# Strassen–Winograd on one core: S3 x T3 multiplied plainly in the first group of the table, T3's sums placed behind it, and a new order for every group

## The chip, the cores and the metric

One core of a Trainium2 chip runs the whole program. The metric is the device time of one execution in microseconds (us); three executions of the kernel before took 1464.37 to 1465.89 us, with a median of 1464.87.

## What is computed

```python
cs = np.cumsum(x, axis=1)
diff = cs - np.concatenate([np.zeros((B, 1, D)), cs[:, :-1, :]], axis=1)
return np.matmul(diff, w).astype(np.float32)   # x: 8 x 2048 x 2048, w: 2048 x 2048
```

A running sum followed by the differences of its neighbours gives x back, so what has to be computed is x times w: 16384 rows of x, cut into 128 tiles of 128 rows, each times a 2048 x 2048 matrix.

## The kernel before, in words

The first 4 tiles are multiplied plainly, the next 4 by one level of Strassen–Winograd, the next 4 by a mixture (`group_half`). From tile 12 on, 29 **groups** of four tiles each are worked through by a table. A group at tile g has the tiles g, h = g+2, k = g+1 and l = g+3. Tile g with tile k, and tile h with tile l, form the two row blocks of a 2 x 2 split: A11 and A12 are the two halves (of K) of g or h, A21 and A22 those of k or l. The matrix w, in 16-bit floats, is split into B11 to B22 and their sums T1 to T4, which stay in SBUF (named W). The seven outer products of a group are

- P1 = A11 x B11, P2 = A12 x B21, P3 = S4 x B22, P4 = A22 x T4, P5 = S1 x T1, P6 = S2 x T2, P7 = S3 x T3,
- where S1 = A21+A22, S2 = S1-A11, S4 = A12-S2, S3 = A22-S2, made in place by VectorE (DVE, L563, 128x1024).

P6 is multiplied plainly (L573): 32 matmuls in eight steps, P6g.0 to P6g.3 for tile g and P6h.0 to P6h.3 for h. The other six are split once more in the manner of Strassen–Winograd: seven quarter products `p1` to `p7` of 4 matmuls each (L592), 28 in place of 32, at the price of small sums of x (`s1` to `s4`, 128x512; six of them a group, listed in `ON_POOL`, run on POOL at L561, the others on DVE at L563), of copies on ScalarE (ACT, L1054, L1086), of merges in PSUM (`m1`, `a5g` and so on, L1061, DVE) and of sums of W. Those sums of W either lie ready (made once by `less`, L555, 128x2048) or are made anew in every group in a tile named flow by a *fill* (`fp4`, `fp5`..., L958, DVE). A group is 6 x 28 + 32 = 200 matmuls of 128x512.

T3's inner products need two sums that are made once, in place, on T3's own memory: T3 quarter 12 less quarter 11, then quarter 22 less that. In the kernel before both are made in the first group just ahead of P7's first fill.

The results of a product are read out of PSUM by `keep` (ACT, L600 with the row's scale, L1116 without) and later products are added by `add` (DVE, L603 with the scale, L1127 without). `last` (ACT, L600) then applies the scale where `add` did not, and `put` (L614) sends the 128x512 piece out. A tile of x comes in by `load` (L113, two transfers of 512 KB), its sizes are taken by `weigh0`, `weigh1` (ACT, L125), `scale` (POOL, L142), `recip` (DVE, L156), `unit` (POOL, L161), it is narrowed to 16 bits by `narrow0`, `narrow1` (ACT, L172) and transposed by two transfers, `turn0`, `turn1` (L185). All loads, turns and almost all puts are issued by SyncE (SP), in order.

What stands where on each engine is set by the string `ORDER`: 215 names, each with an offset of the group to which it belongs. For every group the loop goes through the string and issues each step to its engine; each engine then works in that order and waits by semaphores. Buffers (banks of PSUM, pieces c, the four scratch tiles of small sums) are handed out in that order as well. A load's two buffers are shared with the tile two places before it in the queue g, h, k, l, so load.k waits for turn1.g to land, load.l for turn1.h.

Of the kernel before, what the change touches and what calls it, by code (L numbers as in the profile page):

```python
# [10 lines left out]
def kernel(  # L11
# [1255 lines left out]
    ORDER = """  # L1267
    S1.h+0 S2.h+0 last.C12h1-1 put.C21h1-1 put.C12h1-1 last.C11g1+0 S4.h+0 keep.C22g0+0
    P3.p2+0 P6h.3+0 P5.s1+0 keep.C12g0+0 weigh0.g+1 add.C12g0.z+0 P6h.0+0 P6h.2+0
    P6h.1+0 weigh1.g+1 add.C11h0.q+0 S3.g+0 P5.s3+0 keep.C12g1+0 P7.p1+0 P4.p1+0  # L1270
    put.C11g1+0 P7.fp5+0 P3.s1+0 put.C11h0+0 S3.h+0 scale.g+1 recip.g+1 P7.s1+0 P7.c1+0
    P3.s3+0 P7.s2+0 put.C11h1+0 P7.a1+0 narrow0.g+1 P7.s3+0 P7.p5+0 P7.s4+0 P7.p6+0
    P7.p2+0 P7.fp7+0 keep.C12h1+0 P5.s2+0 P7.c5+0 P5.p5+0 keep.C21g0+0 P7.c6+0
    add.C22g0.x+0 P7.a5g+0 narrow1.g+1 P4.s1+0 P7.a5h+0 P5.s4+0 P5.ct+0 P7.a6+0 load.h+1
    P7.p7+0 P4.p2+0 add.C21g0.x+0 P4.s2+0 P5.p6+0 turn0.g+1 put.C21g0+0 P7.c7+0 P7.p3+0
    P3.s2+0 weigh0.h+1 P3.p1+0 P5.m1+0 P5.p3+0 weigh1.h+1 P7.a7h+0 put.C22g0+0
    add.C12g0.q+0 P5.fp4+0 P5.p7+0 last.C12g0+0 P3.s4+0 turn1.g+1 P3.p6+0 P4.p6+0
    keep.C22g1+0 P5.m2+0 P5.p4+0 scale.h+1 unit.l+0 add.C22g1.x+0 recip.h+1
    add.C12g1.q+0 keep.C12h0+0 P3.p7+0 P3.p3+0 P7.a7k+0 narrow0.h+1 keep.C22h0+0
    put.C12g0+0 keep.C22h1+0 narrow1.h+1 P7.fp4+0 add.C12h1.q+0 add.C12h0.q+0  # L1280
    add.C12h1.z+0 add.C22h1.x+0 P4.s3+0 unit.g+1 P7.p4+0 keep.C21h1+0 P3.p4+0 P4.p5+0
    P4.s4+0 add.C12h0.z+0 P3.p5+0 put.C22g1+0 keep.C21g1+0 P4.fp4+0 add.C12g1.z+0
    add.C22h0.x+0 add.C12g1.e+0 load.k+1 P4.p3+0 last.C12h0+0 weigh0.k+1 turn0.h+1
    P2.p1+1 P1.p1+1 weigh1.k+1 last.C12g1+0 turn1.h+1 P1.cg+1 add.C21g1.x+0 P1.s1+1
    scale.k+1 recip.k+1 put.C22h0+0 narrow0.k+1 put.C22h1+0 P4.p4+0 P1.s2+1 P1.p5+1
    add.C21g1.q+0 P1.s4+1 P2.s1+1 add.C21h1.e+0 P1.ct+1 put.C12h0+0 P2.s2+1 narrow1.k+1
    P1.p6+1 put.C12g1+0 keep.C11g0+1 P1.m1+1 P4.p7+0 add.C21h1.q+0 P1.p2+1 P1.s3+1
    P1.p3+1 load.l+1 P1.p7+1 unit.h+1 unit.k+1 P1.fp4+1 last.C21g1+0 keep.C21h0+0
    P2.s4+1 turn0.k+1 add.C21h0.x+0 P1.m2+1 keep.C11g1+1 P2.p6+1 add.C11g1.q+1 P2.cv+1
    weigh0.l+1 keep.C11h1+1 P2.s3+1 P2.p2+1 P2.p5+1 weigh1.l+1 P1.p4+1 add.C11g0.v+1  # L1290
    add.C11h1.e+1 turn1.k+1 last.C21h1+0 P2.p7+1 scale.l+1 put.C21h0+0 recip.l+1
    add.C12h1.e+0 S1.g+1 P2.p3+1 P5.p1+1 narrow0.l+1 S2.g+1 P2.fp4+1 P6g.0+1 P6g.1+1
    add.C11h1.q+1 narrow1.l+1 P2.p4+1 add.C11g1.e+1 P5.cg+1 P5.p2+1 put.C21g1+0
    put.C11g0+1 S4.g+1 P3.fp2+1 turn0.l+1 keep.C11h0+1 turn1.l+1 load.g+2 last.C11h1+1
    P6g.3+1 P6g.2+1
    """
# [72 lines left out]
```

## Time and profile before

| | us |
|---|---|
| median of three runs | 1464.87 |
| the profiled execution, whole | 1463.69 |
| its span (first to last instruction) | 1461.9 |
| PE busy, 6563 matmuls | 1428.8 |
| DVE busy, 2367 instructions | 1408.8 |
| ACT busy | 1160.6 |
| POOL busy | 356.6 |
| granted clock of TensorE over the span | 0.996 |

The profiled execution is 1.2 us shorter than the median of the runs and 1.8 us longer than its span. In the timeline a row merges neighbours of one kind; the figure behind x is how many, and a bracket tells how long the engine was idle before the row and who ended the wait. Times of a row count from the span's start. The table's 29 groups fill it from about 170 us on.

### The profile page before, as it was taken

What the parts mean: (1) busy time and instruction counts of PE and PEld (TensorE: products, weight loads), DVE (VectorE), ACT (ScalarE), POOL (GpSimd) and SP (SyncE); (2) the same over time, 40 slices, a digit from 0 to 9 for tenths busy, and PEclk for the clock granted to TensorE, in tenths of its full rate; (3) what the DMA queues carried; (4) which work ended last, traced back from release to release, by engine and by line L of the source; (5) the groups of instructions that cost most, each with busy time, mean ns of one, the idle gap of its engine ahead of it and who ended that gap; (6) DMA issues with size and microseconds to landing.
All of it is one profiled execution on the core that took longest, in us unless ns stands there. A gap on an engine that the chain in (4) does not pass through costs nothing. (4 is left out here: it accounts for less than half of the span.)

```text
span 1461.9 us, 21138 instructions
## 1 busy us (share of the span) xinstructions
PE 1428.8 (98%) x6563; PEld 635.8 (43%) x6563; DVE 1408.8 (96%) x2367; ACT 1160.6 (79%) x1786; POOL 356.6 (24%) x422
## 2 busy tenths in 40 slices
PE   8999989999999999999999999999999999999997
PEld 3444434444444444444444444444444444444443
DVE  7998899999999999999999999999999999999998
ACT  5887558888788888887888888887888887788882
POOL 0111021223231223321223321222321223221221
PEclk9999999999999999999999999999999999999999
DMA  9999839999898989889998899998889999889992
GB/s 358 368 237 298 213 121 237 240 232 252 228 244 232 250 228 251 236 237 239 238 238 247 238 230 251 251 228 240 241 239 239 252 229 243 229 245 245 248 243 105
DMA packets 377761, 351.65 MB, mean 241 GB/s; under 512 B 274800, under 2 KB 274800, under 8 KB 377520
## 3 DMA queue, kind: packets, MB, share of 16 engines
q1 hardware_dynamic: 377088, 348.47, 88.0%
q0 software_dynamic: 560, 1.84, 0.3%
q8 instruction: 51, 0.84, 0.2%
q14 instruction: 62, 0.51, 0.1%
HBM read 150.99 MB, written 134.22 MB: 195 GB/s over the span
## 5 line engine op out<-in xcount | busy, mean ns | idle before, releaser
L592 PE MATMUL b<-W,x 128*128 128x512 f16 x2124 | 522.3, 380 | 8.2 <-DVE x L563 6.1
L592 PEld LDWEIGHTS <-x 128*128 128x128 f16 x2952 | 286.5, 98 | 372.3 <-DVE x L563 19.6
L1127 DVE TENSOR_TENSOR c<-b,c 128x512 f32<-128x512 f32 x504 | 332.6, 678 | 0.6 <-issue 0.3
L172 ACT ACTIVATE F<-F,of 128x1024 f16<-128x1024 f32 x246 | 283.0, 1150 | 32.6 <-DVE of L156 30.8
L125 ACT ACTIVATE waste<-F 128x1024 uint8<-128x1024 f32 x246 | 259.9, 1057 | 54.5 <-DMA F<-in_x_dram 51.8
L592 PEld LDWEIGHTS <-inner 128*128 128x128 f16 x1996 | 192.6, 98 | 250.3 <-DVE inner L563 27.2
L592 PE MATMUL b<-W,inner 128*128 128x512 f16 x1176 | 288.9, 380 | 1.1 <-DVE inner L563 0.5
L573 PE MATMUL b<-W,x 128*128 128x512 f16 x1216 | 278.0, 379 | 0.3 <-DVE x L563 0.2
L563 DVE TENSOR_TENSOR x<-x,x 128x1024 f16<-128x1024 f16 (+1 forms) x359 | 211.9, 597 | 9.6 <-DMA x<-F 6.3
L603 DVE SCALAR_TENSOR_TENSOR c<-b,of,c 128x512 f32<-128x512 f32 x286 | 209.6, 740 | 8.9 <-PE b L592 5.5
L592 PE MATMUL b<-flow,x 128*128 128x512 f16 x820 | 210.4, 379 | 5.3 <-DVE flow L958 4.3
L600 ACT ACTIVATE c<-b,of 128x512 f32<-128x512 f32 x268 | 178.1, 681 | 37.9 <-PE b L592 13.7
L142 POOL TENSOR_SCALAR of<-of 128x1 f32<-128x1 f32 x112 | 79.5, 710 | 470.1 <-ACT waste L125 412.5
L1061 DVE TENSOR_TENSOR b<-b,c 128x512 f32<-128x512 f32 x290 | 191.6, 687 | 0.2 <-PE b L592 0.2
L1116 ACT COPY c<-b 128x512 f32<-128x512 f32 x224 | 128.5, 579 | 71.4 <-DVE c L603 45.0
L958 DVE TENSOR_TENSOR flow<-W 128x2048 f16<-128x2048 f16 x145 | 184.2, 1270 | 0.0
L573 PEld LDWEIGHTS <-x 128*128 128x128 f16 x1216 | 118.6, 98 | 144.7 <-DVE x L563 7.1
L600 ACT ACTIVATE c<-c,of 128x512 f32<-128x512 f32 x224 | 154.8, 714 | 12.9 <-DVE c L1127 12.9
L592 PE MATMUL b<-inner 128*128 128x512 f16 x472 | 121.1, 379 | 0.0
L561 POOL TENSOR_TENSOR inner<-x 128x512 f16<-128x512 f16 x29 | 35.7, 1232 | 268.2 <-PE b L592 268.2
L561 POOL TENSOR_TENSOR x<-x,x 128x512 f16<-128x512 f16 x58 | 88.3, 1522 | 22.3 <-PE b L592 22.3
L1086 ACT COPY c<-b 128x512 f32<-128x512 f32 x116 | 68.2, 588 | 26.8 <-PE b L592 17.9
(78 smaller groups left out, 988.9 us busy)
## 6 DMA issues: line engine op xcount, KB each, us to landing
F<-in_x_dram SPq DMA_DIRECT2D x246, 512.0 KB, 5.8
out_dram<-c SPq DMA_DIRECT2D x492, 256.0 KB, 3.2
W<-in_w_dram SPq DMA_DIRECT2D x32, 512.0 KB, 9.7
W<-in_x_dram SPq DMA_DIRECT2D x16, 256.0 KB, 7.1
x<-F SPq DMA_TRANSPOSE x246, 3.5
...
```

The costliest lines, as they stand in the source:

```text
L125: lambda: nc.scalar.activation(waste, where[t][i], ABS, scale=1.0 / ROW, accum_out=sums_of[t][:, i : i + 1],),
L172: lambda: nc.scalar.activation(narrowed(t)[:, ds(i * NH, NH)], where[t][i], COPY, scale=s),
L561: after("pool", lambda: nc.gpsimd.tensor_tensor(dst.all, p.all, q.all, op))
L563: after("dve", lambda: nc.vector.tensor_tensor(dst.all, p.all, q.all, op))
L573: said = nc.tensor.matmul(to[n], a[k], b[k][:, n, :], start=(first and k == 0), stop=(k == KH - 1), skip_group_check=True,)
L592: said = nc.tensor.matmul(to, a[k], b[k], start=(first and k == 0), stop=(k == 3), skip_group_check=True)
L600: after("act", lambda: nc.scalar.activation(c, p, COPY, scale=u))
L603: after("dve", lambda: nc.vector.scalar_tensor_tensor(c, p, u, c, MUL, ADD))
L958: after("dve", lambda: nc.vector.tensor_tensor(in_twos(flow), x, y, op))
L1061: after("dve", lambda: nc.vector.tensor_tensor(t, p, s, ADD))
L1116: after("act", lambda: nc.scalar.copy(to, p))
L1127: after("dve", lambda: nc.vector.tensor_tensor(to, p, to, ADD))
```

## The change

The diff, cut to what decides; of the table two lines of 29 stand for the rest.

```diff
-    ON_POOL = "P3.s1 P3.s4 P4.s1 P4.s3 P4.s4 P5.s4".split()
+    ON_POOL = "P2.s4 P3.s2 P4.s2 P4.s3 P4.s4 P5.s4".split()
...
-            self.small_sums("P7", A("g", 0), A("h", 0), True)
-            self.onto("P7", *x)
+            if self.more:
+                self.small_sums("P7", A("g", 0), A("h", 0), True)
+                self.onto("P7", *x)
+            else:
+                self.whole("P7", T3, half["g"][0], half["h"][0], *x)
...
     ORDER = """
-    S1.h+0 S2.h+0 last.C12h1-1 put.C21h1-1 put.C12h1-1 last.C11g1+0 S4.h+0 keep.C22g0+0
+    weigh0.l+1 keep.C11h1+1 P2.s3+1 P2.p5+1 weigh1.l+1 add.C11g1.q+1 last.C21h1+0
...
-    groups = [Group(g) for g in range(PLAIN + 8, END, 4)]
+    groups = [Group(g, g > PLAIN + 8) for g in range(PLAIN + 8, END, 4)]
...
+    PLAINLY = {
+        "P7.p5": ["P7g.0"],
+        "P7.p6": ["P7g.1"],
+        "P7.p2": ["P7g.2"],
+        "P7.p7": ["P7g.3"],
+        "P7.a7k": ["P7h.0", "P7h.1"],
+        "P7.fp4": ["P7h.2"],
+        "P7.p4": ["P7h.3"],
+    }
...
-first("P7.fp5", "P7.fp7", "P7.p6", "P7.fp4"): sums_of_T3
+"add.C12h1.e": lambda: less(in_7.t12, in_7.t12, in_7.t11)
+"add.C21h1.e": lambda: less(in_7.Q2, in_7.t22, in_7.t12)
```

Group 12, the first of the table, makes P7 with `whole`: 32 plain matmuls in eight steps P7g.0 to P7h.3, which stand where `PLAINLY` says. Its 28 quarter matmuls, four small sums, three fills, six merges and four copies for P7 are gone. Every other group makes P7 as before. `ORDER` is a new arrangement of the same 215 names (it also begins at another point of the circle), and three of the six sums on POOL are others.

What that does to an engine's rows is shown at three places. First DVE in group 12, around the start of P7. Of the rows before, x11 is S4.h, F is a sum of T1 for P5, c5 and c0 are adds, x00 is S3.g; the row of two W (128x4x512 x2) is the pair of T3's sums, flow the fill P7.fp5, and x10, the last row, S3.h.

```order
L563 TENSOR_TENSOR x11_66<-x11_66,x10_65 128x1024
L555 TENSOR_TENSOR F_62<-W_58 128x2048
L563 TENSOR_TENSOR inner_779<-x30_69 128x512
L1127 TENSOR_TENSOR c5_767<-b5_789,c5_767 128x512
L603 SCALAR_TENSOR_TENSOR c0_747<-b6_790,of_1280,c0_747 128x512
L563 TENSOR_TENSOR x00_63<-x21_68,x00_63 128x1024
L555 TENSOR_TENSOR W_58<-W_58 128x4x512
L563 TENSOR_TENSOR x30_69<-x20_67,x30_69 128x512
L555 TENSOR_TENSOR W_58<-W_58 128x4x512 x2
L958 TENSOR_TENSOR flow_783<-W_58 128x2048
L563 TENSOR_TENSOR x10_65<-x31_70,x10_65 128x1024
```

The same place in the changed kernel, from the sum for P5 (F) to add.C22g0.x, the row that reads PSUM bank b0:

```order
L555 TENSOR_TENSOR F_62<-W_58 128x2048
L563 TENSOR_TENSOR inner_779<-x30_69 128x512
L563 TENSOR_TENSOR x11_66<-x11_66,x10_65 128x1024
L563 TENSOR_TENSOR x00_63<-x21_68,x00_63 128x1024
L555 TENSOR_TENSOR W_58<-W_58 128x4x512
L563 TENSOR_TENSOR x30_69<-x20_67,x30_69 128x512
L563 TENSOR_TENSOR inner_779<-inner_779,x20_67 128x512
L563 TENSOR_TENSOR x20_67<-x31_70 128x512
L1128 TENSOR_TENSOR c5_767<-b2_786,c5_767 128x512
L563 TENSOR_TENSOR x10_65<-x31_70,x10_65 128x1024
L156 RECIPROCAL of_1655<-of_1655 128x1
L603 SCALAR_TENSOR_TENSOR c1_751<-b0_784,of_1320,c1_751 128x512
```

T3's pair, the fill and P7's small sums and merges have left this place; T3's sums now stand 17 and 28 rows behind the last row shown, ahead of add.C12h1.e and add.C21h1.e.

Second, ACT in a later group, around the weighing of the next tile k. Before: the last row of C12h0, then weigh0.k and weigh1.k (one row, x2), last.C12g1 (c2), a copy, narrow0.k, a copy, narrow1.k.

```order
L600 ACTIVATE c1_751<-c1_751,of_5848 128x512
L125 ACTIVATE waste_61,of_6317<-F_62 128x1024 x2
L600 ACTIVATE c2_755<-c2_755,of_5750 128x512
L1054 COPY b6_790<-b3_787 128x512
L172 ACTIVATE F_62<-F_62,of_6317 128x1024
L1054 COPY c0_747<-b4_788 128x512
L172 ACTIVATE F_62<-F_62,of_6317 128x1024
```

And now, with last.C12h1 (c5) between the weighings and keep.C21g1, a copy, narrow0.k, a copy, keep.C11g0, last.C12h0 (c4) and narrow1.k behind them:

```order
L600 ACTIVATE c2_755<-c2_755,of_5743 128x512
L125 ACTIVATE waste_61,of_6288<-F_62 128x1024
L600 ACTIVATE c5_767<-c5_767,of_5839 128x512
L125 ACTIVATE waste_61,of_6288<-F_62 128x1024
L1117 COPY c6_771<-b1_785 128x512
L1055 COPY b2_786<-b6_790 128x512
L172 ACTIVATE F_62<-F_62,of_6288 128x1024
L1055 COPY c2_755<-b4_788 128x512
L600 ACTIVATE c3_759<-b0_784,of_6116 128x512
L600 ACTIVATE c4_763<-c4_763,of_5839 128x512
L172 ACTIVATE F_62<-F_62,of_6288 128x1024
```

last.C12g1 has moved from behind both weighings to ahead of them. On SP the order is in both kernels four puts (put.C12g1 the last of them before, the first now), load.l, turn0.k, turn1.k.

Third, DVE in the same group around P7's last fill. Before: the fill P5.fp4, m2, add.C22g1.x, recip.h, add.C12g1.q, a7k, the fill P7.fp4.

```order
L958 TENSOR_TENSOR flow_783<-W_58 128x2048
L1061 TENSOR_TENSOR b2_786<-b3_787,c0_747 128x512
L603 SCALAR_TENSOR_TENSOR c4_763<-b4_788,of_5944,c4_763 128x512
L156 RECIPROCAL of_6221<-of_6221 128x1
L1127 TENSOR_TENSOR c2_755<-b5_789,c2_755 128x512
L1061 TENSOR_TENSOR b1_785<-b1_785,c6_771 128x512
L958 TENSOR_TENSOR flow_783<-W_58 128x2048
```

Now:

```order
L958 TENSOR_TENSOR flow_783<-W_58 128x2048
L156 RECIPROCAL of_6212<-of_6212 128x1
L1062 TENSOR_TENSOR b6_790<-b4_788,c1_751 128x512
L603 SCALAR_TENSOR_TENSOR c6_771<-b3_787,of_5915,c6_771 128x512
L1128 TENSOR_TENSOR c2_755<-b2_786,c2_755 128x512
L1062 TENSOR_TENSOR b7_791<-b7_791,c3_759 128x512
L958 TENSOR_TENSOR flow_783<-W_58 128x2048
```

recip.h has moved to directly behind the first of the two fills; the other rows kept their order.

More of the change, by code (lines that the diff above doesn't have):

```diff
@@ L1274 @@
[L1274 to L1295, printed above, removed]
+    weigh0.l+1 keep.C11h1+1 P2.s3+1 P2.p5+1 weigh1.l+1 add.C11g1.q+1 last.C21h1+0
+    scale.l+1 P2.fp4+1 add.C11h1.e+1 P2.p7+1 recip.l+1 add.C11h1.q+1 add.C21g1.x+0
+    put.C12h0+0 P2.p2+1 S1.g+1 S2.g+1 put.C21h1+0 P2.p3+1 narrow0.l+1 add.C11g1.e+1
@@ new lines @@
+    put.C21g1+0 P7.s2+1 P7.s3+1 P4.p1+1 recip.g+2 keep.C12g1+1 put.C21h0+0 P7.p5+1
+    P7.a1+1 P7.s4+1 load.h+2 P7.fp7+1 P7.c5+1 P7.a5g+1 P7.p6+1 P7.c6+1 P7.p2+1 P5.p5+1
+    P7.p7+1 add.C22g0.x+1 narrow0.g+2 P7.a6+1 P5.s4+1 P7.a5h+1 P3.s1+1 P4.p2+1 P4.s2+1
+    P5.p6+1 put.C22g0+1 keep.C21g0+1 narrow1.g+2 P7.c7+1 P7.p3+1 turn0.g+2 add.C21g0.x+1
+    P3.s3+1 P5.ct+1 P3.p1+1 put.C21g0+1 weigh1.h+2 P5.m1+1 P5.p7+1 P5.p3+1 P3.s2+1
+    weigh0.h+2 P7.a7h+1 P3.s4+1 scale.h+2 add.C12g0.q+1 P5.fp4+1 keep.C22g1+1 recip.h+2
@@ new lines @@
+    P3.p6+1 last.C12g0+1 P4.p6+1 P5.m2+1 unit.g+2 unit.l+1 keep.C12h0+1 keep.C22h1+1
+    add.C22g1.x+1 narrow0.h+2 P5.p4+1 add.C12g1.q+1 P3.p3+1 unit.h+2 P7.a7k+1 P7.fp4+1
+    P3.p7+1 turn1.g+2 put.C12g0+1 P7.p4+1 put.C22g1+1 add.C12h1.z+1 add.C12g1.z+1
+    add.C22h1.x+1 load.k+2 P3.p5+1 P4.s4+1 narrow1.h+2 keep.C22h0+1 turn0.h+2
+    add.C12h1.q+1 add.C12g1.e+1 keep.C21h1+1 last.C12g1+1 weigh0.k+2 P3.p4+1
+    add.C12h1.e+1 turn1.h+2 last.C12h1+1 add.C12h0.q+1 P4.s3+1 add.C22h0.x+1 P4.fp4+1
@@ new lines @@
+    P4.p3+1 P2.p1+2 put.C12g1+1 add.C12h0.z+1 weigh1.k+2 scale.k+2 P1.s1+2 P4.p5+1
+    P1.s3+2 recip.k+2 P1.s2+2 P1.p1+2 put.C22h0+1 keep.C21g1+1 add.C21g1.q+1 P1.cg+2
+    put.C12h1+1 put.C22h1+1 load.l+2 narrow0.k+2 add.C21h1.e+1 P1.s4+2 P4.p4+1 P1.p5+2
+    P1.ct+2 keep.C11g0+2 P1.p6+2 last.C12h0+1 P2.s1+2 P4.p7+1 narrow1.k+2 turn0.k+2
+    P1.m1+2 P2.s2+2 add.C21h1.q+1 P1.p2+2 P1.p7+2 turn1.k+2 keep.C21h0+1 P2.cv+2
+    P1.fp4+2 P1.p3+2 P1.m2+2 unit.k+2 keep.C11g1+2 P2.s4+2 P2.p6+2 P1.p4+2 add.C21h0.x+1
```

36 lines of the change are left out of this document (19 added, 17 removed).

## The prediction

> **What bounds the kernel now.** The page's first part comes first: which engine is full.
>
> ```profile
> span 1461.9 us, 21138 instructions
> PE 1428.8 (98%) x6563; PEld 635.8 (43%) x6563; DVE 1408.8 (96%) x2367; ACT 1160.6 (79%) x1786; POOL 356.6 (24%) x422
> ```
>
> PE and DVE are both full, so the view by stretches comes next: the whole of the table's steady part (from the start of P5.p1 in group 20 to that in group 124, 26 groups), then single groups, then the first.
>
> ```profile
> 279.70:1419.88 1140.18, 1129.49 (x5202) 503.67 (x5201) 1119.54 (x1925) 946.88 (x1483) 308.41 (x364) 1.00 0.91 240
> 411.24:456.10 44.86, 43.34 (x201) 19.43 (x201) 42.88 (x75) 37.62 (x58) 12.22 (x14) 1.00 0.93 237
> 456.10:499.40 43.30, 43.30 (x200) 19.47 (x201) 42.93 (x75) 35.20 (x57) 12.67 (x14) 1.00 0.89 240
> 543.82:587.09 43.27, 43.27 (x201) 19.42 (x201) 42.80 (x75) 36.41 (x58) 12.23 (x14) 1.00 0.94 245
> 191.00:235.50 44.50, 38.41 (x162) 15.85 (x159) 41.61 (x69) 29.00 (x47) 9.57 (x13) 0.92 0.67 182
> ```
>
> Columns: length, then busy time with count of PE, PEld, DVE, ACT, POOL, then granted clock, DMA share and GB/s. An undisturbed group lasts 43.3 us for 200 matmuls, 0.216 us each, and PE never idles; DVE idles 0.4 to 0.5 us in it. So PE sets the pace and DVE has hardly any room. The steady part averages 1140.18 / 26 = 43.85 us a group: 0.55 us a group, 14 us in all, is disturbance. The first group is worse: 162 matmuls where 200 would fit, at a granted clock of 0.92. Who PE waits for is in the view of waits.
>
> ```profile
> PE b L592 <- DVE inner L563: 6.4, 7, 4.3
> PE b L592 <- DVE x L563: 6.1, 8, 1.5
> PE b L592 <- DVE flow L958: 4.3, 8, 0.6
> ```
>
> Columns: us in total, times, longest. Three kinds of wait, 16.8 us of PE's 33; most of the rest lies in the head and the tail, which the change hardly touches.
>
> **Term A, the first group.** The timeline of PE and DVE shows it.
>
> ```profile
> 193.53 1.90 PE L592 MATMUL b<-W,x 128*128 128x512 f16 x8 [0.76 <-DVE x L563]
> 199.72 1.89 PE L592 MATMUL b<-flow,inner 128*128 128x512 f16 x4 [4.29 <-DVE inner L563]
> 201.40 1.91 PE L592 MATMUL b<-W,inner 128*128 128x512 f16 x4
> 206.09 1.03 PE L592 MATMUL b<-flow,x 128*128 128x512 f16 x4
> 215.37 1.02 PE L592 MATMUL b<-W,x 128*128 128x512 f16 x4 [0.28 <-DVE c L1127]
> 217.47 1.02 PE L592 MATMUL b<-flow,x 128*128 128x512 f16 x4 [0.21 <-DVE flow L958]
> 194.86 2.47 DVE L555 TENSOR_TENSOR W<-W 128x2048 f16<-128x2048 f16 x2
> 197.37 1.22 DVE L958 TENSOR_TENSOR flow<-W 128x2048 f16<-128x2048 f16 x1
> 198.51 0.68 DVE L563 TENSOR_TENSOR x<-x,x 128x1024 f16<-128x1024 f16 x1
> 199.58 0.42 DVE L563 TENSOR_TENSOR x<-x,x 128x512 f16<-128x512 f16 x1
> 199.91 0.42 DVE L563 TENSOR_TENSOR inner<-inner,x 128x512 f16<-128x512 f16 x1
> 822.75 1.88 DVE L1061 TENSOR_TENSOR b<-b,c 128x512 f32<-128x512 f32 x3
> ```
>
> At 199.72 PE starts P7.p5 after 4.29 us of idling: DVE first made T3's two sums (2.47 us) and the fill (1.22). Then 16 matmuls take from 199.72 to 206.09, 6.37 us in place of 16 x 0.216 = 3.5: 2.9 us more, in the stretch with the low granted clock. Both go: the plain product needs no sum of T3, no fill and no small sum, only S3.g and two banks. S3.g stands, in the new rows of DVE, 1.2 + 0.4 + 0.7 + 0.7 = 3 us behind S2.h, while PE has P6h's four steps and P4.p1 there (5 x 0.86 = 4.3), so nothing else is late there. The 0.76 ahead of it, for S3.g, falls with it, and the 0.28 and 0.21 as well, since P7 leaves DVE in this group with three fills (197.37 to 198.51, 1.14 each), four small sums (199.58 to 199.91, 0.33) and six merges (three in 1.88, 0.60 apart) less, 8.3 us. Gains: 4.3 + 2.9 + 0.8 + 0.5 = 8.5.
>
> Costs: 32 matmuls for 28, 4 x 0.216 = 0.9. P4.p2 follows P7g.3 directly on PE and adds into bank b0, which add.C22g0.x must read in between: one DVE add and two hand-overs.
>
> ```profile
> L603 DVE SCALAR_TENSOR_TENSOR c<-b,of,c 128x512 f32<-128x512 f32 x286 | 209.6, 740 | 8.9 <-PE b L592 5.5
> L600 ACT ACTIVATE c<-b,of 128x512 f32<-128x512 f32 x268 | 178.1, 681 | 37.9 <-PE b L592 13.7
> ```
>
> 0.74 and, for the hand-overs, an estimate of some 0.07 each (in the rows of term B a 0.7 us sum starts at 455.35 and PE, released by it, at 456.10), so 0.9. T3's sums are still made, 2.47 us, at the seam to the next group, where DVE can't have saved up the 8.3 us, because it reads what PE has just made. Bounds: 0 (hidden) to 2.5 (nothing hidden); nearest is the row of 543.82, whose DVE idles 0.47 us, so I take 1.7. A = -8.5 + 0.9 + 0.9 + 1.7 = **-5.0** (-6.7 to -4.2).
>
> **Term B, waits for tile k.** The 6.1 us behind "x L563" are, but for the 0.76 above, P5.p1 waiting for S1.g.
>
> ```profile
> 456.10 1.04 PE L592 MATMUL b<-W,x 128*128 128x512 f16 x4 [1.52 <-DVE x L563]
> 455.35 1.42 DVE L563 TENSOR_TENSOR x<-x,x 128x1024 f16<-128x1024 f16 x2 [1.51 <-DMA x<-F]
> 444.43 1.01 SPq L113 DMA_DIRECT2D F<-in_x_dram  x2
> 445.60 5.29 SPq L185 DMA_TRANSPOSE x<-F  x2
> L125 ACT ACTIVATE waste<-F 128x1024 uint8<-128x1024 f32 x246 | 259.9, 1057 | 54.5 <-DMA F<-in_x_dram 51.8
> ```
>
> DVE waited 1.51 us for k's transposes, PE 1.52 for DVE. SP issues load.l (1 MB) at 444.43 and both of k's turns right behind it, which take it 5.29 us: the transposes queue behind the load. In the new rows of ACT last.C12g1 stands ahead of two weighings of 1.06 us, so put.C12g1, ahead of load.l on SP, is free some 2 us earlier, the load with it, and k's transposes land earlier by up to as much; the string also names turn1.k six PE steps (5.2 us) ahead of S1.g, before one. No wait was over 1.52. Value: all of it, -(6.1 - 0.8) = **-5.3**; bounds 0 to -5.3.
>
> **Term C, the fill that meets a sum on POOL.** 4.3 us behind "flow" and 6.4 - 4.3 - 0.5 = 1.6 behind "inner" (0.5 is of the first group's start) are left, less 0.2 counted in A: 5.7.
>
> ```profile
> 371.97 2.15 DVE L563 TENSOR_TENSOR x<-x,x 128x1024 f16<-128x1024 f16 x3 [0.73 <-DMA x<-F]
> 391.61 2.09 DVE L958 TENSOR_TENSOR flow<-W 128x2048 f16<-128x2048 f16 x1
> 391.46 1.15 POOL L561 TENSOR_TENSOR x<-x,x 128x512 f16<-128x512 f16 x1 [0.50 <-PE b L592]
> 393.75 1.02 PE L592 MATMUL b<-flow,x 128*128 128x512 f16 x4 [0.65 <-DVE flow L958]
> 831.31 1.21 DVE L958 TENSOR_TENSOR flow<-W 128x2048 f16<-128x2048 f16 x1
> 831.34 2.20 POOL L561 TENSOR_TENSOR x<-x,x 128x512 f16<-128x512 f16 x1 [0.66 <-PE b L592]
> ```
>
> P7.fp4 on DVE and P4.s4 on POOL are let go by one and the same product, P5.p4. Where DVE starts no later (831.31), its fill takes 1.21 and POOL's sum 2.20. Where POOL is 0.15 ahead (391.46), the sum takes 1.15, the fill 2.09, and PE waits 0.65. DVE was late there because it had waited 0.73 us for tile l's transposes. In the new string turn1.l stands three PE steps ahead of S1.h, before two: 0.9 us more. That covers the 0.73 of this group, but the pair still starts on one event. Value: half, **-2.8**; bounds -5.7 and, where the fill loses more often, the rival below.
>
> [...]
>
> **Term D, undisturbed groups.** 43.3 us against 200 x 0.216 = 43.2: 0.1 us a group, 2.6 in all, can be won. What could be lost are DVE's own waits.
>
> ```profile
> DVE of L156 <- POOL of L142: 8.5, 35, 1.0
> ```
>
> `recip` waits for `scale` 8.5 us in all. In the new rows recip.h stands directly behind a fill, and load.h behind four puts, so it may wait anew; recip.g and recip.k now have sums of x between them and their `scale`. Bounds -2.6 and +2.6 (0.1 us a group either way); I take **+1.0**. ACT (79%), POOL (24%) and the tail's own fixed order are left at nothing; ACT's cover is the 5 to 8 us that it idles in a group.
>
> **Sum.** -5.0 - 5.3 - 2.8 + 1.0 = -12.1 on the profiled execution's 1463.69, 1451.6; the median lies 1.2 above that execution, so **1452.8**.
>
> **Rivals.**
> - *All waits of the table go*: A, B, all of C, D's 2.6: -5.0 - 5.3 - 5.7 - 2.6 = -18.6, 1446.3. For it: every one of them begins with a late transpose. Against: the pair on one event.
> - *Only the first group counts*: the transposes land as late as before, because DMA is at a share of 0.91 anyway: -5.0 + 1.0, 1460.9.
> - *The fill loses in every group*, the one that ends slower. The new rows put the chain P5.p3, keep.C22g1 (ACT, 0.68), add.C22g1.x, add.C12g1.q, a7k ahead of P7.fp4: 0.68 + 0.66 + 0.60 + 0.60 + two hand-overs 0.1 = 2.64 us from the end of P5.p3, while PE ends P5.p4 3 x 0.86 = 2.59 us after it. DVE and POOL are within 0.1 us of each other; from about 0.1 behind POOL's start DVE loses. It decides from about 20 lost groups on: 4.3 / 0.65, six waits, are there already, and 22 more of the 28 groups that keep the fill are 14.3, with C at nothing: -5.0 - 5.3 + 1.0 + 14.3 = +5.0, 1469.9. Against it: both wait for the same product, and a DVE that is there in time starts first (831.31 against 831.34), as it did in all but six groups.
> - *Half of them lose*: near 1462 to 1466, no change that a measurement shows (within 0.2%, 2.9 us, is about what one can tell here).
>
> **How the numbers follow.** Forecast 0.48, its own range 1447 to 1459; all waits go 0.14; only the first group 0.14; half lose 0.09; all lose 0.15. Faster by over 0.2%: 0.48 + 0.14 + 0.14 = 0.76; within: 0.09; slower: 0.15. The range runs from 1443, below the second case by its bounds, to 1468, into the cases where most fills lose, short of all of them: some 0.14 lies above, 0.04 below.
>
> **What would show it.** A: no wait over 1 us in group 12, no stretch with a granted clock of 0.92, a wait of about 0.9 ahead of P4.p2, and one of 1 to 2 us in all behind T3's sums. B: no wait of "x L563" for DMA at S1.g. C: the number of fills of 2.1 us at P7.fp4, six before; the slow rival needs over 20. D: undisturbed groups of 43.2 to 43.4 us. Wrong would be, above all, a group that lasts over 43.8 us with no late transpose in it.

## The result, and the profile after

The changed kernel took **1496.98 us** (median of 4 executions, 1495.37 to 1499.84), the kernel before on the same chip 1465.09 (1464.37 to 1465.89): a ratio of 1.0222, 95% interval 1.0203 to 1.024, 31.9 us slower. 1452.8 was predicted, and the range ended at 1468. The profiled execution took 1495.37, its span is 31.4 us longer than that of before. The page's first part:

```profile
span 1493.3 us, 21071 instructions
PE 1439.1 (96%) x6567; PEld 632.1 (42%) x6567; DVE 1424.4 (95%) x2354; ACT 1147.4 (77%) x1782; POOL 406.8 (27%) x422
```

DVE has 13 instructions fewer than before and is busy 15.6 us longer; POOL has as many as before and is busy 50 us longer. Somebody's instructions have become slower. Where, the view by stretches tells: the steady part (P5.p1 of group 20 to that of group 124), group 72, group 80, and the first group, now from its own P5.p1 to the next group's. Columns as in the prediction.

```profile
276.20:1453.59 1177.39, 1142.47 (x5201) 500.72 (x5201) 1145.22 (x1925) 936.19 (x1483) 353.49 (x364) 1.00 0.89 233
867.55:912.76 45.21, 43.91 (x201) 19.27 (x201) 44.44 (x75) 36.09 (x58) 13.50 (x14) 1.00 0.88 233
957.14:1002.38 45.24, 43.78 (x201) 19.28 (x200) 43.64 (x75) 35.93 (x58) 13.65 (x14) 1.00 0.89 233
183.47:231.31 47.84, 44.99 (x205) 19.74 (x204) 38.97 (x65) 33.24 (x52) 11.60 (x13) 1.00 0.65 177
```

The first group in the same stretch of the kernel before:

```profile
182.25:235.50 53.25, 47.16 (x202) 19.86 (x200) 49.27 (x78) 34.78 (x56) 11.08 (x13) 0.94 0.57 157
```

The first group is 5.4 us shorter. The steady part is 1177.39 - 1140.18 = 37.2 us longer, 45.28 us a group for 43.85. (The rest: head +1.2, the second group +0.7, the tail -2.3; in all 31.4.) DVE's share of it, with the same 1925 instructions: busy 1145.22 for 1119.54, **25.7 us more**; idle 32.2 for 20.6, **11.5 us more**. Both halves have to be explained. The view of PE's waits, columns us in total, times, longest:

```profile
PE b L592 <- DVE flow L958: 19.2, 29, 1.0
PE b L592 <- ACT c L1087: 9.6, 20, 1.1
PE b L592 <- DVE b L1062: 7.5, 16, 0.7
PE b L592 <- DVE inner L563: 1.6, 3, 0.6
PE b L592 <- DVE x L563: 0.4, 2, 0.2
```

The three kinds of before are nearly gone but for the fill, 8 times before and now 29; two new ones stand beside it. (A step's last matmul is drawn 0.17 us longer than the 0.86 us at which steps follow each other, so each wait costs some 0.17 us more than this view says.) Counted in the two traces from the start of one step to the start of the next, PE's steps of the steady part come 54.2 us late in all, for 17.0 before: the 37.2 us. Of them P7.p4 has 16.2 (21.1 for 4.9), P7.p6 12.5 and P5.p7 7.5, which lost nothing before; P5.p1 gives 5.3 back (2.9 for 8.2); the other 6.3 are small waits, most of them too short for the view. One group shows all three in a row. Here is group 72, DVE first, from P3.s3 to P7's last fill; a row without a bracket follows its predecessor without idling.

```profile
885.51 1.37 DVE L563 TENSOR_TENSOR x<-x,x 128x512 f16<-128x512 f16 x1
886.80 1.28 DVE L1062 TENSOR_TENSOR b<-b,c 128x512 f32<-128x512 f32 x2
888.00 0.41 DVE L563 TENSOR_TENSOR inner<-x,inner 128x512 f16<-128x512 f16 x1
888.33 0.68 DVE L1128 TENSOR_TENSOR c<-b,c 128x512 f32<-128x512 f32 x1
888.93 1.21 DVE L958 TENSOR_TENSOR flow<-W 128x2048 f16<-128x2048 f16 x1
...
891.98 0.68 DVE L1062 TENSOR_TENSOR b<-b,c 128x512 f32<-128x512 f32 x1
892.58 1.76 DVE L958 TENSOR_TENSOR flow<-W 128x2048 f16<-128x2048 f16 x1
```

POOL, PE and ACT beside it:

```profile
885.44 1.16 POOL L561 TENSOR_TENSOR inner<-inner,x 128x512 f16<-128x512 f16 x1 [1.05 <-PE b L592]
892.10 3.25 POOL L561 TENSOR_TENSOR x<-x,x 128x512 f16<-128x512 f16 x2 [1.56 <-PE b L592]
887.54 1.02 PE L592 MATMUL b<-W,x 128*128 128x512 f16 x4 [0.46 <-DVE b L1062]
890.99 1.03 PE L592 MATMUL b<-flow,x 128*128 128x512 f16 x4
894.39 1.02 PE L592 MATMUL b<-flow,x 128*128 128x512 f16 x4 [0.65 <-DVE flow L958]
876.19 1.06 ACT L125 ACTIVATE waste<-F 128x1024 uint8<-128x1024 f32 x1 [1.97 <-DMA F<-in_x_dram]
879.37 0.58 ACT L1087 COPY c<-b 128x512 f32<-128x512 f32 x1
880.00 1.02 PE L592 MATMUL b<-W,inner 128*128 128x512 f16 x4 [0.18 <-ACT c L1087]
885.58 0.60 ACT L1055 COPY c<-b 128x512 f32<-128x512 f32 x1
```

- 885.44: POOL's P3.s2 starts 0.07 us ahead of DVE's P3.s3 (885.51), which then takes 1.37 us in place of 0.42. That makes P5.m1 (886.80) late, and PE waits 0.46 for it at P5.p7 (887.54). So in 13 of the 27 groups between the first and the last.
- 886.80 to 892.58: from P5.m1 on DVE works without a break for 5.78 us and reaches the fill P7.fp4 at 892.58. PE let it and POOL's P4.s4 go at 892.02 (the end of P5.p4, 890.99 + 1.03). POOL started at 892.10; the fill takes 1.76 for 1.21 and PE waits 0.65. So in all 27 groups.
- 876.19: ACT had waited 1.97 us for load.g; the copy c1 (879.37), behind two weighings and two other rows, is late for PE's P7.p6 (880.00), which waits for c1 in most groups.

Of DVE's 25.7 us the rows by shape account for most: the 128x512 sums of x, of which P3.s3 is one in three, and the fills that read sums of T, one in five of them P7.fp4.

```profile
L563 DVE TENSOR_TENSOR x<-x,x 128x512 f16<-128x512 f16 x89 | 49.3, 555 | 0.1
L958 DVE TENSOR_TENSOR flow<-W 128x2048 f16<-128x2048 f16 x142 | 187.7, 1322 | 0.0
```

Before these groups had a mean of 415 and 1270 ns: 89 x 0.14 = 12.5 us and 142 x 0.052 = 7.4 us more. Of the 11.5 us of idling, 7.4 are DVE's waits for copies of ACT such as c1 (20 times, none before) and 1.7 more waits of recip. Whether these stretched rows are the cause, or only what a late DVE looks like, the trace alone does not say.

### The profile page after: what moved, and what is told of

Same layout as the page of the kernel before. It is cut to its first block, busy times and chain, and to the rows that moved or that the text cites. A ratio compares the mean times of both kernels' runs of the same rounds, so it can differ in the third digit from the quotient of the medians.

```text
span 1493.3 us, 21071 instructions
## 1 busy us (share of the span) xinstructions
PE 1439.1 (96%) x6567; PEld 632.1 (42%) x6567; DVE 1424.4 (95%) x2354; ACT 1147.4 (77%) x1782; POOL 406.8 (27%) x422
## 4 chain that ended last, share of the span: by engine, by line
PE 39%; DVE 25%; DMA 14%; ACT 10%; issue 9%; POOL 2%; SPq 1%; DVEq 0%; ACTq 0%
PE b L592 27%; PE b L573 9%; DVE c L1128 7%; DVE flow L958 6%; DMA out_dram<-c 6%; DMA F<-in_x_dram 5%; DVE b L1062 4%; ACT waste L125 4%; DVE c L603 3%; ACT c L600 3%; DVE x L563 2%; PE b L289 2%; DVE inner L563 2%; POOL of L142 2%; DMA W<-in_w_dram 2%
## 5 line engine op out<-in xcount | busy, mean ns | idle before, releaser
L592 PEld LDWEIGHTS <-inner 128*128 128x128 f16 x1984 | 188.6, 98 | 262.4 <-DVE inner L563 27.5
L600 ACT ACTIVATE c<-b,of 128x512 f32<-128x512 f32 x268 | 181.8, 684 | 81.5 <-PE b L592 44.6
L142 POOL TENSOR_SCALAR of<-of 128x1 f32<-128x1 f32 x112 | 64.2, 573 | 659.7 <-ACT waste L125 548.0
L592 PE MATMUL b<-flow,x 128*128 128x512 f16 x812 | 208.2, 379 | 20.5 <-DVE flow L958 19.2
L563 DVE TENSOR_TENSOR x<-x,x 128x1024 f16<-128x1024 f16 (+1 forms) x329 | 209.4, 651 | 5.9 <-DMA x<-F 3.6
L1117 ACT COPY c<-b 128x512 f32<-128x512 f32 x224 | 129.8, 580 | 84.2 <-DVE c L603 47.1
L958 DVE TENSOR_TENSOR flow<-W 128x2048 f16<-128x2048 f16 x142 | 187.7, 1322 | 0.0
L600 ACT ACTIVATE c<-c,of 128x512 f32<-128x512 f32 x224 | 160.3, 716 | 17.1 <-DVE c L1128 17.1
L561 POOL TENSOR_TENSOR inner<-x,inner 128x512 f16<-128x512 f16 x58 | 108.3, 1867 | 174.7 <-PE b L592 164.8
L561 POOL TENSOR_TENSOR x<-x,x 128x512 f16<-128x512 f16 x87 | 127.3, 1477 | 52.6 <-PE b L592 46.4
L161 POOL TENSOR_SCALAR of<-of,uw 128x1 f32<-128x1 f32 x124 | 65.6, 545 | 91.6 <-DVE of L147 81.4
```

The lines of the kernel that those rows point to most:

```text
L561: after("pool", lambda: nc.gpsimd.tensor_tensor(dst.all, p.all, q.all, op))
L563: after("dve", lambda: nc.vector.tensor_tensor(dst.all, p.all, q.all, op))
L592: said = nc.tensor.matmul(to, a[k], b[k], start=(first and k == 0), stop=(k == 3), skip_group_check=True)
L600: after("act", lambda: nc.scalar.activation(c, p, COPY, scale=u))
L958: after("dve", lambda: nc.vector.tensor_tensor(in_twos(flow), x, y, op))
L1117: after("act", lambda: nc.scalar.copy(to, p))
```

## The experiments

The expectations name the theories by letters. M: rows of DVE and POOL meet and stretch each other. Q: ACT waits for load.g, and DVE is late from the copy c1 on. K: the unbroken chain of DVE rows from P5.m1 to P7.fp4 is too long, so the fill loses. T: the new string loses the fills whatever POOL does. D: DVE is full, and a wait that is taken away comes back elsewhere. A: ACT is late because of load.g. The runs are numbered in the order in which they ran. Moves in the string are shown as a difference of its names. All ratios are to the kernel before on the same chip, with the 95% interval.

**1. Only the first group.** The string and POOL's list of before, with the plain first group; its steps and T3's sums stand where the old string leaves room. The lines are a difference to the changed kernel, without the string and the list.

```diff
         "P7.p6": ["P7g.1"],
-        "P7.p2": ["P7g.2"],
-        "P7.p7": ["P7g.3"],
+        "P7.p2": ["P7g.2", "P7g.3"],
         "P7.a7k": ["P7h.0", "P7h.1"],
-        "P7.fp4": ["P7h.2"],
-        "P7.p4": ["P7h.3"],
+        "P7.fp4": ["P7h.2", "P7h.3"],
...
-"add.C12h1.e": lambda: less(in_7.t12, in_7.t12, in_7.t11)
+"add.C12g1.e": lambda: less(in_7.t12, in_7.t12, in_7.t11)
```

> The table and the POOL sums of before; only the first group multiplies S3 x T3 plainly, with T3's sums behind it. Both theories expect the 4.29 us wait and the half-rate stretch of the first group to go: group 12 (P5.p1 to P5.p1 of the next) 53.3 us before, about 48 here, and the run about 5 us (0.3%) faster than before. If the first group's gain is paid back at the seam, the run is within 0.1% of before.

1457.51 us, ratio 0.9955 [0.994, 0.9971]: 6.6 us faster than the kernel before. The first group, and the steady part:

```profile
182.39:229.43 47.04, 44.79 (x206) 19.64 (x204) 39.48 (x65) 32.63 (x52) 10.63 (x13) 1.00 0.67 179
273.00:1413.91 1140.91, 1129.95 (x5201) 503.79 (x5201) 1118.19 (x1925) 947.43 (x1483) 307.92 (x364) 1.00 0.90 240
```

53.25 has become 47.04, the granted clock 1.00, and the other groups are as they were (1140.91 for 1140.18). The plain first group is a gain; everything lost is lost by the new order and the new list.

**5 and 6. The string alone, the list alone.** Run 5 is the changed kernel with the old list:

```diff
-    ON_POOL = "P2.s4 P3.s2 P4.s2 P4.s3 P4.s4 P5.s4".split()
+    ON_POOL = "P3.s1 P3.s4 P4.s1 P4.s3 P4.s4 P5.s4".split()
```

> The changed kernel with the six POOL sums of the kernel before: the new string and the plain first group stay. Theory K (the chain on DVE): what loses the fills P7.fp4 is the chain from P5.m1 to P7.fp4, 5.48 us of DVE rows in the kernel before against 6.04 us in which PE comes from P5.p6 to the end of P5.p4; P3.s4, moved from POOL into it, makes it 5.81, and P3.s3, stretched by POOL's P3.s2, starts it late. With the old list P3.s4 is off the chain and P3.s2 off POOL: most fills are won, P7.p4 waits under 6 us in all, P5.p7 under 2, the time 1465 to 1476. Theory T (the string alone): copies on ACT come late whatever POOL does, the fills are lost as before, P7.p4 waits about 20 us, 1485 or more.

Run 6 is the kernel before with the new list:

```diff
-    ON_POOL = "P3.s1 P3.s4 P4.s1 P4.s3 P4.s4 P5.s4".split()
+    ON_POOL = "P2.s4 P3.s2 P4.s2 P4.s3 P4.s4 P5.s4".split()
```

> The kernel before with the six POOL sums of the changed kernel: the old string, no plain first group. Theory K: P3.s4 on DVE leaves 0.2 us of the 0.56 spare, so fills are lost in most groups: P7.p4 waits 12 to 20 us in all, 1475 to 1485. Theory T: the list alone does little, within 4 us of 1465.

1497.45 (1.0235 [1.0212, 1.0259]) and 1499.86 us (1.0254 [1.0236, 1.0273]): **either half alone costs as much as both**, and either alone loses every fill. Of run 6:

```profile
PE b L592 <- DVE flow L958: 19.1, 29, 0.7
PE b L592 <- DVE b L1061: 7.4, 30, 1.1
279.00:1456.64 1177.64, 1141.40 (x5200) 499.52 (x5201) 1147.23 (x1925) 940.81 (x1483) 303.39 (x364) 1.00 0.87 233
```

Run 6 bears K out in the lost fills (P3.s4 has joined the chain), but its time lies 15 us above K's range: P7.p3 waits for a merge in every group as well (the second line), which I had not foreseen. Run 5 went as T said, but not against K: I had overlooked that with the old list the new string puts P3.s2 on DVE right behind P5.m1, inside the chain, where the old string has it ahead of P5.m1. In all three kernels the chain is one 0.33 us sum longer than before. How thin the margin of the kernel before is, its own rows show: the chain starts with this row, and ends at the fill of 831.31, 0.03 us ahead of POOL's sum (831.34).

```profile
825.87 1.29 DVE L1061 TENSOR_TENSOR b<-b,c 128x512 f32<-128x512 f32 x2
```

5.44 us, against 5.78 in group 72 of the changed kernel. In another group of before POOL's sum starts first, by 0.05 us, and the fill still takes its 1.21:

```profile
304.14 2.28 POOL L561 TENSOR_TENSOR x<-x,x 128x512 f16<-128x512 f16 x1 [0.59 <-PE b L592]
304.19 1.21 DVE L958 TENSOR_TENSOR flow<-W 128x2048 f16<-128x2048 f16 x1
```

In the 26 groups of the steady part of before the fill starts from 0.05 us ahead of POOL's sum to 0.06 behind it and is won (20 times), or 0.14 behind it and is lost (six times); where it starts ahead, it follows the row before it at most 0.06 us later than a row follows another without waiting. One sum more, 0.33, is more than all of that together.

**2. P3.s3 out of POOL's way.** The changed kernel with P3.s3 behind P3.s4.

```diff
-P3.s3+1
 P5.ct+1
...
 P3.s4+1
+P3.s3+1
```

> The changed kernel with one name moved: P3.s3 stands behind P3.s4, so that the POOL sum P3.s2 has only readers of PSUM beside it on DVE. Theory M (POOL and DVE meet): P3.s3 stays at 0.42 us, the waits of P5.p7 for m1 (8.0 us) go, DVE reaches P7.fp4 earlier in the 12 groups concerned: about 1480 to 1489 us, fewer than 28 lost fills. Theory Q (ACT is late behind load.g, DVE late from c1 on): no more than the 8 us go, all 28 fills stay lost: about 1489 to 1492.

1489.19 us, 1.0172 [1.0148, 1.0196]. No P3.s3 is stretched any more, P5.p7's waits are gone, DVE is 13.5 us less busy in the steady part (1131.68 for 1145.22), but only 7 us come back:

```profile
276.12:1448.64 1172.52, 1142.43 (x5202) 500.69 (x5201) 1131.68 (x1925) 937.12 (x1483) 350.47 (x364) 1.00 0.90 233
PE b L592 <- DVE flow L958: 19.2, 29, 1.0
```

DVE now idles 0.44 us a group at P5.m1, for the copy ct on ACT, and the fills are lost as before. The move also puts P3.s3 into the chain, one more sum of 0.33 us, so by K this run could not win them. That M is not what loses the fills is shown by the changed kernel itself: they are lost as well in the 14 groups in which P3.s3 is not stretched. So M alone does not do.

**3. c1 earlier on ACT.** The changed kernel with weigh1.g, and scale.g and recip.g that depend on it, behind P7.c1.

```diff
-weigh1.g+2
-scale.g+2
...
 P7.c1+1
+weigh1.g+2
+scale.g+2
...
-recip.g+2
...
 P7.s4+1
+recip.g+2
```

> The changed kernel with weigh1.g and scale.g moved on ACT and POOL to behind P7.c1, and recip.g on DVE to behind P7.s4. Theory Q: the waits of P7.p6 (12.5 us) go, DVE is no longer late by 0.7 to 1.1 us at a1, and P7.fp4 is in time again: about 1465 to 1475 us. Theory M: only the 12.5 us go, the fills stay lost: about 1484.

1522.91 us, 1.0415 [1.0387, 1.0443]: a miss. P7.p6 waits less, but weigh1.g now holds up c5 and c6, PE's waits for fills rise from 19.2 to 28.8 us (48 times: P7.fp7, behind a recip.g that now waits for scale.g, meets POOL's P5.s4 as well), and P3.s3 is stretched more often.

**4. P4.s4 back on DVE, P4.s1 on POOL in its place.**

```diff
-    ON_POOL = "P2.s4 P3.s2 P4.s2 P4.s3 P4.s4 P5.s4".split()
+    ON_POOL = "P2.s4 P3.s2 P4.s1 P4.s2 P4.s3 P5.s4".split()
```

> The changed kernel with P4.s4 on DVE and P4.s1 on POOL in its place: as many sums on each engine, but no POOL sum is let go by the product that lets P7.fp4 go. Theory M: fills of 1.22 us, the waits of P7.p4 (21.9 us) go: about 1475 us. Theory Q: DVE is late there in any case, the fill's start does not move and P7.p4 still waits: only the 0.55 us of stretch per group are won, about 1482.

1497.28 us, 1.0227 [1.0199, 1.0255]. No fill is stretched (1.22 us), PE's waits for fills fall from 19.2 to 7.4 us, and the time does not move, as D has it. From start to start P7.p4 loses 7.0 us for 21.1, but P4.p4, which lost nothing, loses 8.7 for its own fill P4.fp4, one sum later on DVE now, P5.p7 and P7.p6 lose 21.0 for 20.0, and the rest are smaller waits.

**7 and 15. A shorter chain.** add.C22g1.x (0.66 us) behind the fill:

```diff
-add.C22g1.x+1
...
 P7.fp4+1
+add.C22g1.x+1
```

> The changed kernel with add.C22g1.x moved from the chain to right behind P7.fp4. Theory K: 0.66 us less ahead of the fill; it starts before POOL's P4.s4, takes 1.22, P7.p4 waits under 6 us in all in place of 21.9, 1478 to 1484. Theory D (DVE has nothing to spare in the new string): the fills may be won but the time goes to other waits, or DVE is later than 0.66 us anyway: over 1490.

1539.38 us, 1.0523 [1.0506, 1.0541]. Every fill is won and P7.p4 waits no more, as K has it, and yet it is the dearest edit so far. The new wait, of DVE's P1.s1 for transposes:

```profile
DVE inner L563 <- DMA x<-F: 29.8, 28, 2.4
```

put.C22g1 needs the sum that was put off; on SP load.k, turn0.h and turn1.h stand behind it. Run 15 lets load.k pass:

```diff
 load.k+2
+put.C22g1+1
```

> The seventh experiment's kernel (add.C22g1.x behind P7.fp4) with load.k ahead of put.C22g1 on SP. If the seventh lost its time because put.C22g1, held up by the later add, held load.k and with it turn1.h back, P1.p5's 30.8 us go and the time falls by about 30 us, to 1505 to 1512 (K: to under 1490, since the fills are won). Rival: the DMA engines are late whatever the order on SP, over 1530.

1499.64 us, 1.0249 [1.0233, 1.0265]: 40 us back, so nearly all that run 7 lost beside the changed kernel was SP's queue. But with all fills won the time is still that of the changed kernel.

**9 and 12. Another row out of the chain.** Run 9 puts add.C12g1.q of the changed kernel behind the fill, run 12 that of run 1. (In run 12 that sum reads its bank only after P3.p7 has added to it, so column 1 of C12 in tile g is another sum.)

```diff
-add.C12g1.q+1
...
 P7.fp4+1
+add.C12g1.q+1
```

> The changed kernel with add.C12g1.q, one of the rows between P5.m1 and P7.fp4 on DVE, moved to right behind P7.fp4. No put hangs on it directly, unlike add.C22g1.x, which the seventh experiment moved. Theory K (the chain on DVE loses the fills): the fill starts some 0.6 us earlier, ahead of POOL's P4.s4, takes 1.22 us, and P7.p4 waits under 5 us in all in place of 21.9; POOL's sum takes 2.19 and may make P4.p4 or P3.p5 wait, up to 11 us as in the seventh: 1476 to 1488. Theory D (DVE has nothing to spare, a wait taken away comes back elsewhere): P7.p4 falls, but the new waits are as long, 1490 or more.

> The first experiment's kernel with add.C12g1.q moved behind P7.fp4. Theory K: the four or so fills that are still lost there are won too, P7.p4's 3.2 us goes, 1454 to 1455. Theory D: POOL's sum, now always the stretched one, or the add, now 1.9 us later, makes another step wait in every group: 1460 or more.

1499.76 (1.025 [1.0226, 1.0275]) and 1466.72 us (1.0017 [1.0005, 1.003]). In run 9 the fills are won and P7.p4's waits gone, but PE's next step adds into the bank that the delayed sum still has to read:

```profile
PE b L592 <- DVE c L1128: 29.3, 29, 1.1
```

In run 12 there is no such wait; DVE comes early to the fill and idles there, 12 us in all, and PE waits as long at P1.p5, 0.4 us in every group: 9 us worse than run 1. A row that is put off costs its time later, where DVE has none.

**13 and 14. The same number of rows, no meeting at the fill.** P4.s4 to DVE, P3.s4 to POOL:

```diff
-    ON_POOL = "P2.s4 P3.s2 P4.s2 P4.s3 P4.s4 P5.s4".split()
+    ON_POOL = "P2.s4 P3.s2 P3.s4 P4.s2 P4.s3 P5.s4".split()
```

> The changed kernel with two sums exchanged: P4.s4 from POOL to DVE, P3.s4 from DVE to POOL; DVE has as many rows as before. No sum of POOL can meet the fill P7.fp4, and P3.s4 (0.33 us) is off the chain from P5.m1 to P7.fp4. Theory K (the fills lost to POOL by a late chain are what the change costs most): P7.p4 waits under 4 us in all in place of 21.9, nothing stands in for it, 1472 to 1480. Theory D (DVE is full in the new string, a wait taken away there comes back as others): within 6 us of 1497, with new waits behind P4.s4 and the rows after it.

1488.63 us, 1.0175 [1.016, 1.019], by the ratios 7 us below the changed kernel and between the two expectations.

```profile
PE b L592 <- DVE b L1062: 9.7, 19, 1.4
PE b L592 <- ACT c L1087: 8.3, 17, 1.5
PE b L592 <- DVE flow L958: 3.5, 13, 1.3
277.32:1450.39 1173.07, 1147.73 (x5202) 500.45 (x5201) 1135.26 (x1925) 936.56 (x1483) 326.05 (x364) 1.00 0.91 233
```

The fills cost 3.5 us for 19.2 and DVE is 10 us less busy, but its idle time has grown from 32.2 to 37.8: of the 16 us that PE no longer waits for fills, 7 come back (K), the rest goes to other waits (D), 7.7 us of it, from start to start, to P4.p4: its fill P4.fp4 ends 0.3 us late in every group, a wait of at most 0.17 by the view. Run 14 also takes last.C21g1 from ahead of c1:

```diff
-last.C21g1+0
...
 P7.c1+1
+last.C21g1+0
```

> As e13_s4_swap, and on ACT last.C21g1 behind P7.c1 in place of ahead of it, the pieces handed out as before. If c1 is late because it queues behind rows that wait for load.g, it comes 0.7 us earlier, P7.p6 waits 5 to 9 us less in all and the time is 4 to 8 us under e13. Rival: put.C21g1, now later, holds load.h or a piece back, same time or slower.

1560.51 us, 1.067 [1.0643, 1.0697]. put.C21g1 goes out later, and the copy c5 waits for its piece; P7.p6, at which the move aimed, still loses 8.4 us for 10.5:

```profile
ACT c L1087 <- DMA out_dram<-c: 76.9, 50, 2.9
```

**10. Run 9 with c1 ahead of last.C21g1 and keep.C12h1.**

```diff
-last.C21g1+0
...
-keep.C12h1+1
...
 P7.c1+1
+keep.C12h1+1
+last.C21g1+0
```

> As the ninth, and on ACT P7.c1 ahead of last.C21g1 and keep.C12h1, which stood between weigh1.g and it. If c1's place behind rows that wait for load.g is what P7.p6 waits for, P7.p6 falls from 12.5 us in all to under 3, and the time is 8 to 11 us below the ninth's. Rival: as in the third experiment, what was put behind c1 is late in its turn (keep.C12h1 holds a bank of PSUM, last.C21g1 holds put.C21g1 and load.h back), within 3 us of the ninth or slower.

1569.21 us, 1.0728 [1.0705, 1.0752]. From start to start P7.p6's waits fall from 9 to under 2 us, as Q has it; the price is the same wait for a piece (73.1 us).

**17. ACT's narrowing out of the way.** Run 2 with narrow1.g (1.15 us) behind ct.

```diff
-narrow1.g+2
 P7.c7+1
...
 P5.ct+1
+narrow1.g+2
```

> The second experiment's kernel (the changed one with P3.s3 behind P3.s4), and on ACT narrow1.g behind P5.ct in place of ahead of it. Theory A (ACT late behind load.g): in the second experiment DVE idled 0.44 us in every group at P5.m1, which waits for the copy ct; ACT reaches ct late because it had waited 2 us for load.g and then had no break. With narrow1.g (1.15 us) out of the way m1 starts some 0.5 us earlier, so does the fill P7.fp4, which then wins: m1's waits under 3 us in all, P7.p4 under 6 in place of 21.9, 1470 to 1478. Theory D: within 5 us of the second experiment's 1489, with new waits elsewhere.

1488.77 us, 1.0181 [1.0168, 1.0194]: no change to run 2. P5.m1 does start earlier (its idling falls from 11.8 to 3.6 us in all), but the fill does not, because of a row in between:

```profile
883.46 1.21 DVE L958 TENSOR_TENSOR flow<-W 128x2048 f16<-128x2048 f16 x1
884.86 0.16 DVE L156 RECIPROCAL of<-of 128x1 f32<-128x1 f32 x1 [0.19 <-POOL of L142]
887.38 1.64 DVE L958 TENSOR_TENSOR flow<-W 128x2048 f16<-128x2048 f16 x1
```

recip.h, which the new string has directly behind the fill P5.fp4, waits for scale.h and that for weigh0.h, and narrow1.g stands ahead of weigh0.h on ACT as before. In run 2 DVE came too late to wait there; now it waits 0.19 us in every group. ACT holds the chain up in two places, and freeing one leaves the other.

**8 and 11. Term B by itself, on run 1.** Run 8 moves last.C12g1 on ACT to where the new string has it, run 11 load.l on SP ahead of put.C12g1.

```diff
 last.C12h0+0
+last.C12g1+0
 weigh0.k+1
 weigh1.k+1
-last.C12g1+0
```

> The old string with the plain first group (as in the first experiment), and last.C12g1 moved on ACT from behind the two weighings of tile k to ahead of them, as the new string has it. If term B's reason holds (put.C12g1 holds load.l back on SP, load.l the transposes of k), P5.p1 waits under 3 us in all in place of 8.1, and the time is 1451 to 1454. Rival: the transposes land as late as before, since they queue behind all other transfers: P5.p1 stays at 7 to 9, 1457.

```diff
+load.l+1
 put.C12g1+0
...
-load.l+1
```

> The first experiment's kernel (old string, plain first group) with load.l ahead of put.C12g1 on SP, so that the load no longer waits for last.C12g1, and ACT and DVE keep their rows. If term B's reason holds, load.l goes out 0.6 us earlier, the transposes of k land that much earlier, the waits of S1.g for DMA (2.7 us in all) go, and P5.p1 waits 2 to 3 us less in all: 1454 to 1456. Rival: DVE's own lateness, not the transposes, makes the rest of P5.p1's waits, and the time is that of the first, 1457 to 1458.

1517.67 (1.0376 [1.0355, 1.0396]) and 1529.98 us (1.0455 [1.0428, 1.0482]). Both do to P5.p1 what term B says: it starts 3.2 and 1.1 us late in all, in place of 8.1 in run 1. And both pay for it many times over, in these rows of run 8 and of run 11:

```profile
DVE of L156 <- POOL of L142: 72.9, 49, 2.5
```

```profile
ACT c L1117 <- DMA out_dram<-c: 67.7, 27, 3.9
```

In run 8 last.C12g1 waits 1.9 us for DVE ahead of weigh0.k, so recip.k comes 2.5 us late in every group; and, in run 11, a put.C12g1 behind load.l keeps its piece from keep.C11g1.

**16 and 18. On the kernel that beats both.** Run 1 with P4.s4 and P4.s2 exchanged, and run 1 with a seventh sum on POOL.

```diff
-    ON_POOL = "P3.s1 P3.s4 P4.s1 P4.s3 P4.s4 P5.s4".split()
+    ON_POOL = "P3.s1 P3.s4 P4.s1 P4.s2 P4.s3 P5.s4".split()
```

> The first experiment's kernel (old string, plain first group) with P4.s4 on DVE and P4.s2 on POOL: the sum that meets the fill P7.fp4 leaves POOL, DVE has as many rows. Theory K: the four lost fills are won, 1454 to 1456. Theory D: one of the two exchanged sums makes another step late in every group, 1460 or more.

```diff
-    ON_POOL = "P3.s1 P3.s4 P4.s1 P4.s3 P4.s4 P5.s4".split()
+    ON_POOL = "P2.s4 P3.s1 P3.s4 P4.s1 P4.s3 P4.s4 P5.s4".split()
```

> The first experiment's kernel (old string, plain first group) with a seventh sum on POOL, P2.s4, 0.34 us a group less on DVE; in the sixth experiment this sum made no row of DVE longer. If DVE's rows plus its waits set the pace (43.18 + 0.70 us a group in the first), a group lasts 43.5 to 43.7 in place of 43.88 and the time is 1449 to 1454. Rival: the sum takes 1.85 us on POOL and holds scale.l back, so recip.l waits (0.25 us a group in the sixth), or PE waits for the sum itself: 1456 or more.

1461.92 (0.9996 [0.9985, 1.0006]) and **1454.86 us (0.9946 [0.9933, 0.9959])**. In run 16 no fill is lost, but P3.s2 on DVE, right behind P4.s2's start on POOL, is stretched from 0.42 to a mean of 0.76, and P1.p5 is 0.3 us late in every group. In run 18 DVE is 7 us less busy than in run 1 (1110.92 for 1118.19), and half of the 26 groups run at PE's pace, 43.3 us or less (5 of them in run 1):

```profile
272.23:1411.50 1139.27, 1129.30 (x5201) 504.87 (x5201) 1110.92 (x1899) 945.07 (x1483) 356.64 (x390) 1.00 0.91 241
577.16:620.36 43.20, 43.20 (x202) 19.42 (x202) 42.58 (x74) 36.40 (x58) 13.77 (x15) 1.00 0.93 244
```

The steady part is only 1.6 us shorter than run 1's, since DVE's idling rises by 5.6: what is left are PE's pace, late transposes and a few lost fills. The two intervals overlap, so run 18 beats both kernels, but that it beats run 1 is not shown.

## Why the prediction was wrong, point by point

- **Term A, right.** Predicted -5.0; alone it measured -6.6 (run 1). In the changed kernel the idling of 4.29 us and the low clock are gone, P4.p2 waits as foreseen (198.96, 0.63 and the 0.17 that the view leaves out, for 0.9), and behind T3's sums stand the other two waits below, 1.7 by the view and 2.0 with the 0.17 each; the 1.7 of the prediction was a choice between 0 and 2.5.

```profile
198.96 1.02 PE L592 MATMUL b<-W,x 128*128 128x512 f16 x4 [0.63 <-DVE c L603]
218.06 1.02 PE L592 MATMUL b<-flow,x 128*128 128x512 f16 x4 [0.98 <-DVE flow L958]
223.33 1.89 PE L592 MATMUL b<-W,inner 128*128 128x512 f16 x8 [0.71 <-DVE b L1062]
```

- **Term B, right** in the changed kernel: PE's 6.1 us behind "x L563" are 0.4, and from start to start P5.p1 loses 5.3 us less, as predicted. The way there is the predicted one: against the time at which P5.p1 is due, load.l goes out 11.8 us ahead for 10.0 before and turn1.k lands 2.6 ahead for 1.0 (means of the 26 groups). The sum counted the move as free; in the old string the same move (run 8) and another with the same aim (run 11) cost 60 and 73 us.
- **Term C, the step that failed.** "Value: half, -2.8": 8 waits for a fill before are 29 now, and P7.fp4 loses in every group. The prediction looked at the event that lets the pair go, and in the slow rival at a chain that starts at P5.p3. The chain that decides starts at P5.m1, 5.78 us of DVE rows without a break; the hand-over from PE by way of ACT that I priced was not what DVE waited for. The argument against the rival, that DVE "is there in time" in all but six groups, rested on a start 0.03 us ahead in one group; in seven of the 20 won groups POOL starts first, by up to 0.06 us, and in none had DVE as much to spare as one sum takes.
- **The rival named the event and nearly its price.** It priced 22 lost fills at 14.3 us, with the view's 0.65 each; from start to start one costs 0.81, and P7.p4 loses 16.2 us more. It lacked the stretched P3.s3 (P5.p7, 7.5), the late c1 (P7.p6, 12.5) and the small waits (6.3). And what a wait costs is not what its removal brings: with the fills won, run 13 gains 7 us and runs 9 and 15 nothing; without P3.s3's stretch run 2 gains 7. No run took P7.p6's wait away without a dearer one, so that its 12.5 us can be won is not shown.
- **A meeting left out of the sum.** Term C prices the meeting of DVE and POOL at the fill alone. POOL's P3.s2 meets DVE's P3.s3 as well, in 13 groups of the changed kernel, and 0.42 us becomes 1.37 (885.51).
- **Term D, mis-sized, and ACT "left at nothing".** recip does wait a little more (10.2 us for 8.5), but an undisturbed group of 43.3 us is no longer to be found: groups 72 and 80 last 45.2, and the shortest, group 76 between them (912.76 to 957.14), 44.4. ACT idles 1.97 us for load.g, so c1 comes late; from 882.45 in group 72 on it works without a gap up to ct (885.58), so ct and recip.h have no cover either (runs 2 and 17). The 5 to 8 us that it was to idle in a group lie elsewhere and cover nothing here.

What stays open: the shortest mean group of an edit of the new string is 45.0 us (run 17), though most edits removed the wait that they aimed at. Run 2 takes away P3.s3's stretch, run 17 one late row of ACT, run 13 most of the lost fills; run 13 with either of the others was not run, so whether the new string can come below the old one is not known.
